# A 64-byte-offset layout for split weights, wider key matmuls, two-pass gates and float32r decode sums in a one-core decoder layer

## The chip, the cores and the metric

The kernel runs as one program on one core of one Trainium2 chip. The metric is device microseconds of the execution. A profiled execution gives the trace that is quoted below. Engines are named as the profile names them: PE (TensorE matmuls), PEld (TensorE weight loads), DVE (VectorE), ACT (ScalarE), POOL (GpSimd) and SP (SyncE, which here only issues DMAs).

## The reference

One inference step of a hybrid decoder layer for 256 prompt tokens and 8 sample tokens, 264 token columns in all, model width 2048, float32 throughout:

```python
xn = rmsnorm(x, g_mix)
z = xn @ w_in                       # RG-LRU group, mLSTM group, 4 + 4 gate columns
x = x + concat([y_rg, y_ml]) @ w_out
mk = rmsnorm(mem, g_mem) @ w_k      # 256 memory tokens, 4 heads of 512
mv = rmsnorm(mem, g_mem) @ w_v
q = rmsnorm(x, g_xa) @ w_xa_q       # prompt attends to mk, mv; samples to cache_mem_k, cache_mem_v
x = x + attention(q, k, v) @ w_xa_o
xf = rmsnorm(x, g_ffn)
x = x + (silu(xf @ w_ffn_gate) * (xf @ w_ffn_up)) @ w_ffn_down
y = rmsnorm(x, g_final)
```

Outputs are y for all tokens, the recurrent states, and mk and mv. Each of the 8 sample tokens attends to its own 256 cached keys and values in each of 4 heads: 32 pairs of head and sample.

## The kernel before

Tokens lie along the free dimension and features along the partitions, so an activation is 16 chunks of 128 features by 264 columns. Every large product is made to float32 accuracy from three float32r matmuls: each operand is split into a high part (a float32r copy) and a low part (the rest), and `mm3` (line 175) adds high·high, high weight·low token and low weight·high token into one PSUM bank. The moving operand is the token chunk (264 columns), the stationary one a 128x128 block of weights.

The weights are consumed in an ordered list of steps (`steps`, line 137). One step is one output block of 128 features: 2048 weight columns, 16 chunks, 48 matmuls. A step has a DMA of 1 MB into a raw tile (`load_piece`, line 142; three buffers), two splits of 1024 columns each (`split_half`, line 150: ACT copies raw to `wh`, DVE subtracts to get `wl`; four buffers of each), its matmuls, and an evacuation of the bank by DVE and ACT. The main loop (line 1200) runs, for step i: the load of a later piece, the evacuation of the step before, the split of step i+1, the matmuls of step i, and then side work (`pump`, line 207) until the planner's price clocks of DVE and ACT pass that of PE. Engine order is then made by a scheduler with a timeline of its own; only SP keeps the written order. Each engine works through its own instructions in order.

The steps in order are: 41 of `w_in`, 16 of `w_out`, 16 of `w_q`, 16 of `w_k` and 16 of `w_v` mixed by head, 16 of `w_o`, then the feed-forward part in three portions (gate and up projections 88, down projection 48).

Places that the change touches:

- Activations live in the tag `B` (line 100), 26 buffers. The largest tile that uses it has 4 chunks of 264 columns, so a buffer has 4224 bytes; its four rows of 1056 bytes start at 0, 32, 64 and 96 modulo 256 from the buffer's start, and neighbouring buffers differ by 128 modulo 256. `wh` and `wl` are 4096 bytes apart and a block of weights has 512, so every block starts at the same place modulo 256 (224, by the allocator's addresses).
- Step 8 (`w_in[8]`) holds the 8 gate columns in a block of 128 and takes the usual 48 matmuls; `evac_if` (line 501) reads rows 0 to 3 and 32 to 35.
- `w_k` steps: `proj` with 256 memory tokens, 48 matmuls of 256 columns; `evac_k` (line 986) copies the bank out, sends it to `o_k` and splits it (ACT, DVE).
- `w_v` steps: `pe_v` (line 1000) has the weights as the moving operand, 512 columns, and the memory tokens stationary.
- Decode attention: `dec_k` (line 927) issues on POOL's queue the DMAs of one pair's keys and values (512 KB each), then makes q·k products with one ACT and three DVE instructions into `acc`. `dec_v` (line 948) sums `acc` over the partitions with one float32 matmul against a matrix of ones, does the softmax, and weighs the values in four DVE instructions. Two pairs are under way at a time (`NFL`), and a DMA waits for a free buffer of `B`.
- In the 16 `w_k` steps and the decode work POOL's queue holds only DMA issues.

Of the kernel before, what the change touches and what calls it, by code (L numbers as in the profile page):

```python
# [10 lines left out]
F32 = mybir.dt.float32  # L11
F32R = mybir.dt.float32r
I32 = mybir.dt.int32
AF = mybir.ActivationFunctionType
# [3 lines left out]
P = 128  # L18
D = 2048
KC = D // P  # L20
T = 256
# [4 lines left out]
DFF = 5632  # L26
FPARTS = (16, 16, 12)
EPS = 1e-6
XSCALE = 512.0 ** -0.5
KSCALE = 128.0 ** -0.5  # L30

# [49 lines left out]
def layer_kernel(ctx: ExitStack, tc, xT, memT, vec, wrg, w_in, w_out, w_q, w_k, w_v, w_o,  # L81
# [28 lines left out]
    class Arr:  # L110


        def __init__(self, nb, w=N, dt=F32):
            self.t, self.nb, self.w, self.dt = {}, nb, w, dt
# [6 lines left out]
        def __call__(self, c):  # L121
            return self.tile(c // 4)[:, c % 4, :]

    class HL:
# [3 lines left out]
        def __call__(self, c):  # L128
            return self.h(c), self.l(c)

    NB, NT, NL, NFL = 26, 6, 3, 2
    SLACK = 0.5
    POOLC = (4, 5, 10, 11)
# [2 lines left out]

    steps = []
    LD, LS = 3, 1

    raws, splits = {}, {}  # L140

    def load_piece(i):
        if i >= len(steps) or i in raws:
            return
        src, cols = steps[i][0], steps[i][1]
        r = sb.tile([P, 2048], F32, tag="raw", bufs=3, name=nm("raw"))
        sp.dma_start(r[:, :cols], src)
        raws[i] = r

    def split_half(i, h, parts=1):  # L150
        if i >= len(steps):
            return
        cols = steps[i][1]
        lo, hi = h * 1024, min(cols, (h + 1) * 1024)
        wh = sb.tile([P, 1024], F32R, tag="wh", bufs=4, name=nm("wh"))
        wl = sb.tile([P, 1024], F32R, tag="wl", bufs=4, name=nm("wl"))
        r = raws[i]
        n = (hi - lo) // parts
        with tc.high_priority():
            for o in range(0, hi - lo, n):  # L160
                st["split"] = act.activation(wh[:, o: o + n], r[:, lo + o: lo + o + n], AF.Copy)
                dve.tensor_sub(wl[:, o: o + n], r[:, lo + o: lo + o + n], wh[:, o: o + n])
        splits[i, h] = (wh, wl)

    class W:
        def __init__(self, i):
            self.i = i

        def __call__(self, c, w=P):
            per = 1024 // w  # L170
            wh, wl = splits[self.i, c // per]
            o = (c % per) * w
            return wh[:, o: o + w], wl[:, o: o + w]

    def mm3(ps, a, b, start, stop):
        ah, al = a
# [49 lines left out]
    def bank(tag="mm"):  # L226
        return psm.tile([P, 512], F32, tag=tag, bufs=4, name=nm(tag))
# [3 lines left out]
    make_identity(nc, ident)  # L231
    ones = const.tile([P, P], F32, name="ones")
    dve.memset(ones, 1.0)
    warm_act = const.tile([P, 1], F32, name="warm_act")
    act.activation(warm_act, ones[:, 0:1], AF.Square)

# [14 lines left out]
    def V(name, j=0, w=1):  # L251
        o = _V[name][0] + j
        return vecs[:, o: o + w]
# [567 lines left out]
    proj(w_in[8], rx, evac_if)  # L821
    for j in range(8):
        proj(w_in[9 + j], rx, evac_qk(j))
    for j in range(8):
# [52 lines left out]
    def mem_gen():  # L877
        raw = Arr(KC, T)
        for i in range(4):
            pool_e.dma_start(raw.tile(i), memT[:, i * 4: i * 4 + 4, :])  # L880
        yield STEP
        yield STEP
        acc = ltmp(T)
        for c in range(KC):
            sumsq(acc, raw(c), c == 0)
            yield 0.35
        r = ltmp(T)
        yield STEP
        yield from rstd_from(acc, r, D)
        st["mem"] = HL(KC, T)  # L890
# [36 lines left out]
    def dec_k():  # L927
        for h in range(H):
            while qn["n"] < 4 * h + 4:
                yield STEP  # L930
            for b in range(NS):
                while infl["n"] >= NFL:
                    yield STEP
                infl["n"] += 1
                kc = B([P, 4, T])
                pool_e.dma_start(kc, kcT[h, b])  # L936
                w = sb.tile([P, 516], F32, tag="dw", bufs=2, name=nm("dw"))
                vc = B([P, 4, T])
                pool_e.dma_start(vc, vcT[h, b])
# [5 lines left out]
                pairs.append((h, b, w, vc))  # L945
                yield 1.1

    def dec_v():
        done, cur = 0, None
        while done < H * NS:  # L950
            nxt = None
            if pairs:
                nxt = pairs.pop(0)
                ps = bank("ax")
                pe.matmul(ps[:, :T], ones, nxt[2][:, 0:T], start=True, stop=True)
                nxt += (ps,)
            cur, todo = nxt, cur
            if todo is None:
                yield STEP
                continue  # L960
            h, b, w, vc, ps = todo
            mx, p = w[:, 512:513], w[:, T: 2 * T]
            dve.tensor_reduce(mx, ps[:, :T], axis=AX.X, op=OP.max)
            dve.tensor_scalar(mx, mx, -XSCALE, None, op0=OP.mult)
            act.activation(p, ps[:, :T], AF.Exp, scale=XSCALE, bias=mx, accum_out=ssm[:, h, b: b + 1])
            yield 0.5
            for c in range(4):
                dve.scalar_tensor_tensor(w[:, 0:T], vc[:, c, :], 1.0, p, op0=OP.mult, op1=OP.mult,
                                         accum_out=osm[:, 4 * h + c, b: b + 1])
# [16 lines left out]
    def evac_k(h, j):  # L986
        def f(ps):
            if j == 0:
                kv["k", h] = HL(4, T)
            t = tmp(T)  # L990
            act.activation(t, ps[:, :T], AF.Copy)
            pool_e.dma_start(o_k[:, 4 * h + j, :], t)
            kh, kl = kv["k", h](j)
            act.activation(kh, ps[:, :T], AF.Copy)
            dve.tensor_sub(kl, ps[:, :T], kh.bitcast(F32))
            if j == 3:
                st["att", h] = side(attend(h), 1)
        return f

    def pe_v(h, k4):  # L1000
        def f(i):
            if k4 == 0:
                kv["vps"] = [bank(), bank()]
            w = W(i)
            for c in range(4):
                kc = k4 * 4 + c
                mh, ml_ = rm(kc)
                wh, wl = w(c, 512)
                for tb in range(2):
                    ps = kv["vps"][tb]  # L1010
# [21 lines left out]
    def attend(h):  # L1032
# [42 lines left out]
        for c in range(4):  # L1075
# [9 lines left out]
            dve.tensor_sub(ol[:, T:N], x, oh[:, T:N].bitcast(F32))  # L1085
            yield 0.5

    for h in range(H):
        for j in range(4):
            proj(w_k[4 * h + j], rm, evac_k(h, j), n=T, need=("memg",))  # L1090
# [86 lines left out]
    def load_x(lo, hi):  # L1177
        sp.dma_start(xres[:, lo:hi, :], xT[:, lo:hi, :])  # L1178

    r = sb.tile([P, 2048], F32, tag="raw", bufs=3, name=nm("raw"))  # L1180
    raws[0] = r
    for h in range(4):
        if h < 2:
            load_x(2 * h, 2 * h + 2)
        sp.dma_start(r[:, h * 512: h * 512 + 512], w_in[0][:, h * 512: h * 512 + 512])  # L1185
    for q in range(1, 4):
        load_x(4 * q, 4 * q + 4)
        if q < 3:
# [157 lines left out]
```

## Time and profile before

| what | value |
| --- | --- |
| time, three runs | 1582.69, 1577.44, 1579.3 us; median 1579.3 us |
| profiled execution, first to last instruction (its span) | 1577.6 us; of the profiled execution only this is given, and the lowest timed run, 1577.44, lies at it |
| mean granted TensorE clock | 0.994 |
| PE matmuls in the trace | 12356 (a float32 matmul shows as two) |
| DMA | 207 GB/s mean, 325.97 MB |
| stage: w_k and w_v steps | 486.6 to 697.4 us |
| stage: feed-forward, final norm | 807 us to the end |

In the profile a PE record is the matmul with its pipeline, so records overlap: two that follow each other start about 121 ns apart while each lasts about 284 ns. A line L60 is the recording helper that issues nearly everything, so groups are told apart by their tiles. The chain of waits goes back from the last instruction to what released each step. Times of windows are us from the start of the span.

### The profile page before, as it was taken

The numbers are of one execution on the slowest core, as the hardware profiler recorded it, in microseconds if no ns is written. First come the engines' busy times: TensorE is split into PE (matmuls) and PEld (weight loads), VectorE is DVE, ScalarE is ACT, GpSimd is POOL, SyncE is SP. The second block draws the span as 40 slices with busy tenths as digits, with TensorE's granted clock in tenths as the row PEclk, the third lists the DMA queues.
The fourth block names the chain that finished last, engine by engine and source line by source line (L and its number), as shares of the span: only waits on it lengthen the run. The fifth ranks groups of instructions, "written<-read, shape, count | busy, mean of one in ns | idle before, by whom it ended". The sixth has DMA issues, their size and how long they took to land.

```text
span 1577.6 us, 29752 instructions
## 1 busy us (share of the span) xinstructions
PE 1560.9 (99%) x12356; PEld 1536.0 (97%) x12356; DVE 1047.3 (66%) x2019; ACT 779.2 (49%) x1217; POOL 74.9 (5%) x142
## 2 busy tenths in 40 slices
PE   9999999999999999999999999999999999999997
PEld 9999999999999889989999999999999999999997
DVE  7976878787689999856655555455555554555554
ACT  7465775564445555545444444333444433344463
POOL 0001210001012112000000000000000000000000
PEclk9999999999999999999999999999999999999999
DMA  8445875547689888554545555455445555555452
GB/s 311 154 174 171 303 262 202 189 159 260 247 298 353 314 330 302 178 182 180 187 163 185 188 181 173 182 187 186 174 178 185 188 181 174 180 188 188 153 180 97
DMA packets 55303, 325.97 MB, mean 207 GB/s; under 512 B 6688, under 2 KB 7120, under 8 KB 24448
## 3 DMA queue, kind: packets, MB, share of 16 engines
q1 hardware_dynamic: 39744, 270.68, 47.9%
q0 software_dynamic: 15136, 53.16, 9.2%
q8 instruction: 96, 1.57, 0.4%
q10 hardware_dynamic: 288, 0.23, 0.1%
q14 instruction: 39, 0.32, 0.1%
HBM read 312.78 MB, written 11.28 MB: 205 GB/s over the span
## 4 chain that ended last, share of the span: by engine, by line
PE 97%; ACT 1%; DVE 1%; DMA 0%; issue 0%; SPq 0%; DVEq 0%; ACTq 0%
PE mm L60 92%; PE ax L60 6%; DVE B L60 1%; ACT B L60 1%; DMA xres<-xT 0%; ACT wh L60 0%; ACT L60 0%; DVE wl L60 0%; DVE c L60 0%; DVEq L1323 0%; DVE xres L60 0%; ACT t L60 0%; SPq L1185 0%; ACT rstd L60 0%; SPq L1178 0%
## 5 line engine op out<-in xcount | busy, mean ns | idle before, releaser
L60 PE MATMUL mm<-B,wh 128*128 128x264 f32 (+1 forms) x7520 | 1380.0, 285 | 2.8 <-DVE B L60 2.8
L60 PEld LDWEIGHTS mm<-B,wh 128*128 128x128 f32 x7520 | 1166.8, 189 | 4.4 <-ACT cso L60 2.9
L60 PE MATMUL mm<-B,wl 128*128 128x264 f32 (+1 forms) x3760 | 1066.9, 284 | 1.2 <-DVE wl L60 1.2
L60 ACT ACTIVATE wh<-raw 128x1024 fp32r<-128x1024 f32 (+2 forms) x518 | 538.4, 1041 | 710.1 <-PE mm L60 584.1
L60 DVE TENSOR_TENSOR wl<-raw,wh 128x1024 fp32r<-128x1024 f32 (+2 forms) x518 | 620.7, 1200 | 370.0 <-ACT wh L60 361.8
L60 PEld LDWEIGHTS mm<-B,wl 128*128 128x128 f32 x3760 | 708.8, 189 | 1.6 <-DVE wl L60 1.4
L60 DVE TENSOR_TENSOR t<-mm,rstd 128x264 f32<-128x264 f32 x104 | 44.9, 432 | 57.5 <-PE mm L60 57.5
L60 PE MATMUL mm<-wh,B 128*128 128x512 f32 x256 | 83.0, 398 | 0.0
L60 DVE TENSOR_TENSOR xres<-xres,mm 128x264 f32<-128x264 f32 x80 | 34.3, 428 | 46.5 <-PE mm L60 46.5
L60 PEld LDWEIGHTS mm<-wh,B 128*128 128x128 f32 x256 | 48.4, 189 | 10.5
L60 DVE SCALAR_TENSOR_TENSOR dw<-B,dw 128x256 f32<-128x256 f32 x128 | 53.8, 420 | 3.2 <-ACT dw L60 2.2
L60 PE MATMUL mm<-wl,B 128*128 128x512 f32 x128 | 51.0, 398 | 0.0
L60 PE MATMUL ax<-B,B 128*128 128x256 f32 (+3 forms) x288 | 48.7, 312 | 0.0
L60 DVE SCALAR_TENSOR_TENSOR dw<-B,qsm,dw 128x256 f32<-128x256 f32 x96 | 45.9, 480 | 1.2 <-ACT dw L60 0.6
L60 PEld LDWEIGHTS ax<-B,B 128*128 128x128 f32 x288 | 40.7, 189 | 3.4 <-issue 0.7
L1238 POOL TENSOR_TENSOR B<-B,rstd 128x264 f32<-128x264 f32 x4 | 2.8, 739 | 866.0 <-ACT rstd L60 866.0
L60 ACT ACTIVATE B<-xres,vecs 128x264 fp32r<-128x264 f32 (+1 forms) x64 | 31.2, 504 | 2.5 <-DMA xres<-xT 1.3
L60 ACT ACTIVATE t<-xres 128x264 f32<-128x264 f32 x60 | 23.8, 416 | 15.3 <-DVE xres L60 15.3
L60 PEld LDWEIGHTS mm<-wl,B 128*128 128x128 f32 x128 | 24.1, 188 | 5.1
L936 POOL DMA_DIRECT2D B<-kcT x32 | 17.3, 541 | 209.9 <-DVE B L60 119.3
L60 DVE TENSOR_TENSOR acc_x<-acc_x,t 128x264 f32<-128x264 f32 x59 | 25.3, 428 | 0.8 <-ACT t L60 0.5
L60 DVE SCALAR_TENSOR_TENSOR B<-xres,vecs,B 128x264 fp32r<-128x264 f32 x48 | 22.7, 489 | 4.5 <-ACT B L60 4.5
(152 smaller groups left out, 701.3 us busy)
## 6 DMA issues: line engine op xcount, KB each, us to landing
raw<-w_gu SPq DMA_DIRECT2D x88, 1024.0 KB, 4.8
raw<-w_in SPq DMA_DIRECT2D x40, 1024.0 KB, 4.8
raw<-w_d SPq DMA_DIRECT2D x32, 1024.0 KB, 4.8
raw<-w_out SPq DMA_DIRECT2D x16, 1024.0 KB, 4.8
B<-kcT POOLq DMA_DIRECT2D x32, 512.0 KB, 7.0
raw<-w_q SPq DMA_DIRECT2D x16, 1024.0 KB, 6.6
B<-vcT POOLq DMA_DIRECT2D x32, 512.0 KB, 7.6
raw<-w_k SPq DMA_DIRECT2D x16, 1024.0 KB, 7.2
```

The source lines that it names most:

```text
L60: return f(*a, **k)
L936: pool_e.dma_start(kc, kcT[h, b])
L1238: e.tensor_mul(st["y"](c), st["y"](c), r)
```

## The change

Six edits:

1. Every tile of tag `B` now has 1088 columns (4352 bytes, 17 times 256), with the wanted shape cut out of it by `view`. All buffers so start at one place modulo 256.
2. `wh` and `wl` become one tile `W` of two groups of 1088 columns. A group starts with 16 columns of lead, then has four rows of 264: 128 columns of high part, 128 of low, 8 unused. A row of weights so starts 64 bytes after the token row that it meets, modulo 256, and moves on with it by 32 bytes per chunk. The split writes through a pattern of 2 x 4 x 128.
3. Raw pieces are loaded in halves of 1024 columns, five buffers in place of three whole ones.
4. The gate step has 64 columns of high part and 64 of low in one block of 128, and two matmuls per chunk; `evac_if` adds rows 64 to 67 and 96 to 99 to the results, four DVE instructions more.
5. The memory tokens are kept with high and low part side by side (`Side`), 512 columns; `pe_k` takes one matmul of 512 columns with the high weights and one of 256 with the low weights per chunk. `evac_k` copies one half on ACT, adds the other on DVE, and makes the low part of the key on POOL. `pe_v` reads its 512 moving columns as four rows of 128.
6. The decode sum is split: ACT copies `acc` to a float32r high part, POOL subtracts for the low part (`dr`), and PE sums with two float32r matmuls against `ones_r`. The products with the values are written over the value tile.

```diff
+SLOT = 1088
+ROW = 264
+LEAD = 16
...
-    def B(shape, dt=F32):
-        return sb.tile(shape, dt, tag="B", bufs=NB, name=nm("B"))
+    def B(shape, dt=F32, skip=0):
+        return view(sb.tile([P, SLOT], dt, tag="B", bufs=NB, name=nm("B")), shape, skip)
...
+        def both(self, c):
+            q, j = divmod(c, 2)
+            if q not in self.t:
+                self.t[q] = B([P, 2, 2 * T + 8], F32R, skip=16 * (q % 2))
+            return self.t[q][:, j, : 2 * T]
...
+        for h in range(0, cols, 1024):
+            if (i, h // 1024) not in raws:
+                w = min(1024, cols - h)
+                sp.dma_start(raw_half(i, h // 1024)[:, :w], src[:, h: h + w])
...
+        raws[i, h] = sb.tile([P, 1024], F32, tag="raw", bufs=5, name=nm("raw"))
...
-        wh = sb.tile([P, 1024], F32R, tag="wh", bufs=4, name=nm("wh"))
-        wl = sb.tile([P, 1024], F32R, tag="wl", bufs=4, name=nm("wl"))
+        w = sb.tile([P, 2, SLOT], F32R, tag="W", bufs=4, name=nm("W"))
+        ng = (hi - lo) // 512
+        rows = w[:, 0:ng, LEAD: LEAD + 4 * ROW].rearrange("p g (r x) -> p g r x", x=ROW)
...
-                st["split"] = act.activation(wh[:, o: o + n], r[:, lo + o: lo + o + n], AF.Copy)
-                dve.tensor_sub(wl[:, o: o + n], r[:, lo + o: lo + o + n], wh[:, o: o + n])
+                src, wh = raw[:, g, r, :], rows[:, g, r, 0:P]
+                low = rows[:, g, r, P: 2 * P]
+                if fused:
+                    wh, low, src = wh[:, :, :, 0:64], wh[:, :, :, 64:P], src[:, :, :, 0:64]
+                st["split"] = act.activation(wh, src, AF.Copy)
+                dve.tensor_sub(low, src, wh)
...
+        for o, x in ((64, li), (96, u)):
+            low = R(2)[0:4]
+            dve.tensor_mul(low, ps[o: o + 4, :N], rstd[o: o + 4, :])
+            dve.tensor_add(x, x, low)
...
+            pe.matmul(ps[:, :N], w(c)[0], xh, start=c == 0, stop=False)
+            pe.matmul(ps[:, :N], w(c)[0], xl, start=False, stop=c == KC - 1)
...
+                act.activation(wr[:, 0], acc, AF.Copy)
+                pool_e.tensor_sub(wr[:, 1], acc, wr[:, 0].bitcast(F32))
...
-                pe.matmul(ps[:, :T], ones, nxt[2][:, 0:T], start=True, stop=True)
+                for k, x in enumerate(nxt[4]):
+                    pe.matmul(ps[:, :T], ones_r, x, start=k == 0, stop=k == 1)
...
-            act.activation(t, ps[:, :T], AF.Copy)
+            act.activation(t, ps[:, T:], AF.Copy)
+            dve.tensor_add(t, t, ps[:, :T])
...
-            act.activation(kh, ps[:, :T], AF.Copy)
-            dve.tensor_sub(kl, ps[:, :T], kh.bitcast(F32))
+            act.activation(kh, t, AF.Copy)
+            pool_e.tensor_sub(kl, t, kh.bitcast(F32))
...
+            pe.matmul(ps, wh, st["mem"].both(c), start=c == 0, stop=last, skip_group_check=True)
+            if not last:
+                pe.matmul(ps[:, :T], wl, rm(c)[0], start=False, stop=False, skip_group_check=True)
```

On PE, the first key step, before. A `mm` tile is the PSUM bank; the first name behind the arrow is the moving tokens (two buffers, high and low), the second the weights; `ax_5982` is the sum of one decode pair, placed between.

```order
L60 MATMUL mm_6089<-B_4156,wh_6002 128x256
L60 MATMUL mm_6089<-B_4157,wh_6002 128x256
L60 MATMUL mm_6089<-B_4156,wl_6003 128x256
L60 MATMUL ax_5982<-dw_5914,ones 128x256
L60 MATMUL mm_6089<-B_4156,wh_6002 128x256
L60 MATMUL mm_6089<-B_4157,wh_6002 128x256
L60 MATMUL mm_6089<-B_4156,wl_6003 128x256
```

On PE, the same key step in the changed kernel.

```order
L63 MATMUL mm_6127<-B_4149,W_6038 128x512
L63 MATMUL mm_6127<-B_4149,W_6038 128x256
L63 MATMUL mm_6127<-B_4149,W_6038 128x512
L63 MATMUL mm_6127<-B_4149,W_6038 128x256
L63 MATMUL mm_6127<-B_4156,W_6038 128x512
L63 MATMUL mm_6127<-B_4156,W_6038 128x256
L63 MATMUL mm_6127<-B_4156,W_6038 128x512
L63 MATMUL mm_6127<-B_4156,W_6038 128x256
L63 MATMUL mm_6127<-B_4163,W_6038 128x512
L63 MATMUL ax_6014<-dr_5944,ones_r 128x256
L63 MATMUL mm_6127<-B_4163,W_6038 128x256
```

Three matmuls of 256 columns per chunk have become one of 512 and one of 256, and the decode sum reads `dr`, which POOL writes last; its second matmul stands further down.

On POOL, the queue in the decode work, before: each row is the issue of one DMA of keys (kcT) or values (vcT).

```order
L936 DMA B_5669<-kcT 128x1024
L939 DMA B_5672<-vcT 128x1024
L936 DMA B_5748<-kcT 128x1024
L939 DMA B_5751<-vcT 128x1024
L936 DMA B_5827<-kcT 128x1024
L939 DMA B_5830<-vcT 128x1024
```

On POOL, the same place in the changed kernel.

```order
L998 DMA B_5690<-vcT 128x1024
L994 DMA B_5769<-kcT 128x1024
L1005 TENSOR_TENSOR dr_5522<-dw_5521,dr_5522 128x256
L998 DMA B_5773<-vcT 128x1024
L994 DMA B_5852<-kcT 128x1024
L1005 TENSOR_TENSOR dr_5606<-dw_5605,dr_5606 128x256
L998 DMA B_5856<-vcT 128x1024
L1005 TENSOR_TENSOR dr_5689<-dw_5688,dr_5689 128x256
L1005 TENSOR_TENSOR dr_5772<-dw_5771,dr_5772 128x256
L994 DMA B_5941<-kcT 128x1024
```

The subtraction that makes the low part of one pair's `acc` now stands behind DMA issues of later pairs, each of which can wait for a buffer.

More of the change, by code (lines that the diff above doesn't have):

```diff
@@ L98, in nm, with view @@
         return f"{s}_{uid[0]}"
-    def B(shape, dt=F32):
-        return sb.tile(shape, dt, tag="B", bufs=NB, name=nm("B"))
+    def view(t, shape, skip=0):
+        v = t[:, skip: skip + int(np.prod(shape[1:]))]
+        if len(shape) == 2:
+            return v
+        names = "abcd"[:len(shape) - 1]
+        return v.rearrange(f"p ({' '.join(names)}) -> p {' '.join(names)}",
+                           **{c: int(n) for c, n in zip(names[1:], shape[2:])})
+    def B(shape, dt=F32, skip=0):
+        return view(sb.tile([P, SLOT], dt, tag="B", bufs=NB, name=nm("B")), shape, skip)
     def tmp(w=N, tag="t"):
@@ L129, in __call__, with __init__ @@
             return self.h(c), self.l(c)
+    class Side:
+        def __init__(self):
+            self.t = {}
+        def both(self, c):
[3 more added lines that the diff above has]
+            return self.t[q][:, j, : 2 * T]
+        def __call__(self, c):
+            b = self.both(c)
+            return b[:, :T], b[:, T:]
     NB, NT, NL, NFL = 26, 6, 3, 2
@@ L138, in layer_kernel, with raw_half @@
     LD, LS = 3, 1
+    GATES = 8
     raws, splits = {}, {}
     def load_piece(i):
-        if i >= len(steps) or i in raws:
+        if i >= len(steps):
             return
         src, cols = steps[i][0], steps[i][1]
-        r = sb.tile([P, 2048], F32, tag="raw", bufs=3, name=nm("raw"))
-        sp.dma_start(r[:, :cols], src)
-        raws[i] = r
+        for h in range(0, cols, 1024):
+            if (i, h // 1024) not in raws:
+                w = min(1024, cols - h)
+                sp.dma_start(raw_half(i, h // 1024)[:, :w], src[:, h: h + w])
+    def raw_half(i, h):
+        raws[i, h] = sb.tile([P, 1024], F32, tag="raw", bufs=5, name=nm("raw"))
+        return raws[i, h]
     def split_half(i, h, parts=1):
@@ L154, in split_half @@
         lo, hi = h * 1024, min(cols, (h + 1) * 1024)
-        wh = sb.tile([P, 1024], F32R, tag="wh", bufs=4, name=nm("wh"))
-        wl = sb.tile([P, 1024], F32R, tag="wl", bufs=4, name=nm("wl"))
-        r = raws[i]
-        n = (hi - lo) // parts
-        with tc.high_priority():
-            for o in range(0, hi - lo, n):
-                st["split"] = act.activation(wh[:, o: o + n], r[:, lo + o: lo + o + n], AF.Copy)
-                dve.tensor_sub(wl[:, o: o + n], r[:, lo + o: lo + o + n], wh[:, o: o + n])
-        splits[i, h] = (wh, wl)
+        w = sb.tile([P, 2, SLOT], F32R, tag="W", bufs=4, name=nm("W"))
+        ng = (hi - lo) // 512
+        rows = w[:, 0:ng, LEAD: LEAD + 4 * ROW].rearrange("p g (r x) -> p g r x", x=ROW)
+        raw = raws[i, h][:, : hi - lo].rearrange("p (g r x) -> p g r x", r=4, x=P)
+        pieces = [(slice(0, ng), slice(0, 4))]
+        if parts > 1:
+            pieces = [(slice(g, g + 1), slice(r, r + 8 // parts)) for g in range(ng) for r in range(0, 4, 8 // parts)]
+        fused = i == GATES
+        with tc.high_priority():
+            for g, r in pieces:
+                src, wh = raw[:, g, r, :], rows[:, g, r, 0:P]
[4 more added lines that the diff above has]
+                dve.tensor_sub(low, src, wh)
+        splits[i, h] = w
     class W:
@@ L167, in __init__, with __call__, wide @@
             self.i = i
[L169 to L173, printed above, removed]
+        def __call__(self, c):
+            w, g, o = splits[self.i, c // 8], c % 8 // 4, LEAD + c % 4 * ROW
+            return w[:, g, o: o + P], w[:, g, o + P: o + 2 * P]
+        def wide(self, c):
+            w = splits[self.i, c // 2][:, c % 2, LEAD: LEAD + 4 * ROW].rearrange("p (r x) -> p r x", x=ROW)
+            return w[:, :, 0:P], w[:, :, P: 2 * P]
     def mm3(ps, a, b, start, stop):
@@ L233, in layer_kernel @@
     dve.memset(ones, 1.0)
+    ones_r = const.tile([P, P], F32R, name="ones_r")
+    dve.tensor_copy(ones_r, ones)
     warm_act = const.tile([P, 1], F32, name="warm_act")
@@ L820, in layer_kernel, with pe_gates @@
         proj(w_in[n], rx, evac_rgx(n))
-    proj(w_in[8], rx, evac_if)
+    def pe_gates(i):
+        ps = bank()
+        w = W(i)
+        for c in range(KC):
+            xh, xl = rx(c)
+            pe.matmul(ps[:, :N], w(c)[0], xh, start=c == 0, stop=False)
+            pe.matmul(ps[:, :N], w(c)[0], xl, start=False, stop=c == KC - 1)
+        return ps
+    steps.append((w_in[8], 2048, pe_gates, evac_if, ()))
     for j in range(8):
@@ L889, in mem_gen @@
         yield from rstd_from(acc, r, D)
-        st["mem"] = HL(KC, T)
+        st["mem"] = Side()
         for c in range(KC):
@@ L936, in dec_k @@
                 pool_e.dma_start(kc, kcT[h, b])
-                w = sb.tile([P, 516], F32, tag="dw", bufs=2, name=nm("dw"))
+                w = sb.tile([P, 264], F32, tag="dw", bufs=2, name=nm("dw"))
+                wr = sb.tile([P, 2, T], F32R, tag="dr", bufs=2, name=nm("dr"))
                 vc = B([P, 4, T])
@@ L944, in dec_k @@
                     dve.scalar_tensor_tensor(acc, kc[:, c, :], q[c], acc, op0=OP.mult, op1=OP.add)
-                pairs.append((h, b, w, vc))
+                act.activation(wr[:, 0], acc, AF.Copy)
+                pool_e.tensor_sub(wr[:, 1], acc, wr[:, 0].bitcast(F32))
+                pairs.append((h, b, w, vc, (wr[:, 0], wr[:, 1])))
                 yield 1.1
@@ L960, in dec_v @@
                 continue
-            h, b, w, vc, ps = todo
-            mx, p = w[:, 512:513], w[:, T: 2 * T]
+            h, b, w, vc, _, ps = todo
+            mx, p = w[:, T: T + 1], w[:, 0:T]
             dve.tensor_reduce(mx, ps[:, :T], axis=AX.X, op=OP.max)
@@ L1007, in f @@
                 mh, ml_ = rm(kc)
-                wh, wl = w(c, 512)
+                wh, wl = w.wide(c)
                 for tb in range(2):
-                    ps = kv["vps"][tb]
+                    ps = kv["vps"][tb].rearrange("p (r x) -> p r x", x=P)
                     s = slice(tb * P, tb * P + P)
@@ L1086, in attend, with pe_k @@
             yield 0.5
+    def pe_k(i):
+        ps = bank()
+        w = W(i)
+        for c in range(KC):
+            wh, wl = w(c)
+            last = c == KC - 1
+            if last:
+                pe.matmul(ps[:, :T], wl, rm(c)[0], start=False, stop=False, skip_group_check=True)
+            pe.matmul(ps, wh, st["mem"].both(c), start=c == 0, stop=last, skip_group_check=True)
+            if not last:
+                pe.matmul(ps[:, :T], wl, rm(c)[0], start=False, stop=False, skip_group_check=True)
+        return ps
     for h in range(H):
         for j in range(4):
-            proj(w_k[4 * h + j], rm, evac_k(h, j), n=T, need=("memg",))
+            steps.append((w_k[4 * h + j], 2048, pe_k, evac_k(h, j), ("memg",)))
         for k4 in range(4):
@@ L1178, in load_x @@
         sp.dma_start(xres[:, lo:hi, :], xT[:, lo:hi, :])
-    r = sb.tile([P, 2048], F32, tag="raw", bufs=3, name=nm("raw"))
-    raws[0] = r
     for h in range(4):
@@ L1184, in layer_kernel @@
             load_x(2 * h, 2 * h + 2)
-        sp.dma_start(r[:, h * 512: h * 512 + 512], w_in[0][:, h * 512: h * 512 + 512])
+        r = raws[0, h // 2] if h % 2 else raw_half(0, h // 2)
+        sp.dma_start(r[:, h % 2 * 512: h % 2 * 512 + 512], w_in[0][:, h * 512: h * 512 + 512])
     for q in range(1, 4):
```

2 lines of the change are left out of this document (1 added, 1 removed).

## The prediction

> **What bounds the kernel now.** I read the engine totals first, then the chain of waits, and then what PE itself waits for.
>
> ```profile
> span 1577.6 us, 29752 instructions
> PE 1560.9 (99%) x12356; PEld 1536.0 (97%) x12356; DVE 1047.3 (66%) x2019; ACT 779.2 (49%) x1217; POOL 74.9 (5%) x142
> ...
> 807.26 756.09 PE mm L60 x6233
> ...
> PE mm L60 <- DVE B L60: 2.8, 1, 2.8
> PE ax L60 <- ACT wh L60: 1.4, 1, 1.4
> PE mm L60 <- DVE wl L60: 1.2, 1, 1.2
> ```
>
> The first two rows: PE is busy through 99% of the span, DVE through 66%. The third, from the chain of waits in the feed-forward stage, is one unbroken stretch of 6233 matmuls, and 756.09 / 6233 = 121.3 ns each. The last three are waits of PE (us in all, times, longest); they come to 5.4 us. So the time is a count of matmuls times their spacing, and nothing else ends last for long. An edit helps if it removes matmuls or shortens their spacing, and hurts if it makes PE wait.
>
> The groups by shape (busy us, mean ns of a record) and two ranges over 900 to 1200 us (shortest, median and longest record in ns):
>
> ```profile
> L60 PE MATMUL mm<-B,wh 128*128 128x264 f32 x7008 | 1286.5, 285 | 2.8 <-DVE B L60 2.8
> L60 PE MATMUL mm<-B,wl 128*128 128x264 f32 x3504 | 994.9, 284 | 1.2 <-DVE wl L60 1.2
> L60 PE MATMUL mm<-B,wh 128*128 128x256 f32 x512 | 93.5, 283 | 0.0
> L60 PE MATMUL mm<-wh,B 128*128 128x512 f32 x256 | 83.0, 398 | 0.0
> L60 PE MATMUL mm<-B,wl 128*128 128x256 f32 x256 | 72.0, 281 | 0.0
> ...
> L60 PE MATMUL mm<-B,wl x826: 278/283/289, 899.7 to 1199.9; 128*128 128x264 f32 x166
> L60 PE MATMUL mm<-B,wh x1650: 278/284/290, 899.9 to 1199.8; 128*128 128x264 f32 x184
> ```
>
> A record lasts longer than its spacing because matmuls are pipelined: 284 against 121.3 ns, about 163 ns more. I take that 163 off every record to get a spacing: 120 and 118 ns for the two kinds of 256 columns, 235 for 512. The ranges show that equal matmuls differ by up to 12 ns, with PE never waiting.
>
> **The change part by part.** The sum is made against the profiled execution's span of 1577.6 us; the median, 1579.3, lies 1.7 us above it, which I add at the end.
>
> *Layout (edits 1 and 2).* It touches every 264-column matmul, 16 chunks of three in each step. The relation that the change fixes, weights 64 bytes behind the tokens modulo 256, already occurs in the kernel before: by the allocator's addresses its buffers start at 96 or at 224 and a row is 32 further on, so the third row of a buffer at 96 starts at 160, and the weights, always at 224, stand 64 behind it. I looked for it in the output projection, where high and low tokens both lie in buffers that start at 96.
>
> ```profile
> 727.26 0.41 PE L60 MATMUL mm<-B,wh 128*128 128x264 f32 x2
> ...
> 727.63 0.40 PE L60 MATMUL mm<-B,wh 128*128 128x264 f32 x2
> ...
> 727.99 0.41 PE L60 MATMUL mm<-B,wh 128*128 128x264 f32 x2
> ...
> L60 PE MATMUL mm<-B,wh x2: 281/282/283, 727.6 to 727.7; 128*128 128x264 f32 x2
> L60 PE MATMUL mm<-B,wl x1: 286/286/286, 727.9 to 727.9; 128*128 128x264 f32 x1
> ```
>
> The timeline has that chunk at 727.63, with 0.36 us to the next and 0.37 before it; the two rows below are its three records, 281 + 283 + 286 = 850 ns. Three medians make 2 x 284 + 283 = 851, three means 2 x 285 + 284 = 854. So the fixed relation is worth 1 to 4 ns per chunk; I take 2, since chunks start 0.36 and 0.37 us apart in turn. 10,464 / 3 = 3488 chunks keep three matmuls: 3488 x 2 = **7.0 us less**, ends 3.5 and 14. The trace can't tell whether the relation counts or the address alone; both lead to this chunk. A larger gain is not excluded: one matmul in three falling to the shortest record, 278, would bring 6 x 3488 = 20.9 us.
>
> *Gates (4).* One step of 48 matmuls becomes one of 32: 16 x 0.121 = **1.9 us less**.
>
> *Keys (5).* Before, 512 x 120 + 256 x 118 ns = 91.6 us; after, 256 x 235 + 256 x 118 = 90.4 us: **1.3 us less** before rounding. The low-token half rides in the same pass, so only the few ns that a second matmul costs beyond its columns go. The value steps keep their 384 matmuls; no row shows 512 columns read as four rows of 128, and I take 0, with 11 ns either way (the spread of equal matmuls) for the ends, 4 us.
>
> *Decode sums (6).*
>
> ```profile
> 446.57 1.01 DVE L60 SCALAR_TENSOR_TENSOR dw<-B,qsm,dw 128x256 f32<-128x256 f32 x2
> ...
> 450.18 0.59 PE L60 MATMUL ax<-dw,ones 128*128 128x256 f32 x2
> 450.43 0.47 PE L60 MATMUL mm<-B,wl 128*128 128x264 f32 x1
> 450.74 0.41 PE L60 MATMUL mm<-B,wh 128*128 128x264 f32 x2
> ```
>
> From 450.18 to 450.74 PE starts the sum and one ordinary matmul; 0.56 less 0.12 leaves 0.44 us for a float32 sum. Two float32r matmuls of 256 columns take 2 x 0.119 = 0.238. That is 0.20 less for each of 32 pairs: **6.5 us less**. It holds only while the sum's new operand is ready. Before, `acc` is complete at 447.58 (first row) and the sum starts at 450.18: 2.6 us of cover.
>
> ```profile
> L60 ACT ACTIVATE t<-B 128x256 f32<-128x256 f32 x15 | 5.1, 406 | 0.0
> L1238 POOL TENSOR_TENSOR B<-B,rstd x4: 734/738/746, 1568.8 to 1570.9; 128x264 f32<-128x264 f32 x4
> L60 DVE SCALAR_TENSOR_TENSOR t<-t,t 4x264 f32<-4x264 f32 x8 | 3.3, 418 | 0.2
> L60 ACT ACTIVATE wh<-raw 128x1024 fp32r<-128x1024 f32 x496 | 525.7, 1061 | 700.0 <-PE mm L60 574.6 <-issue 105.9 <-ACT B L60 13.9
> L60 DVE TENSOR_TENSOR wl<-raw,wh 128x1024 fp32r<-128x1024 f32 x496 | 606.9, 1225 | 369.2 <-ACT wh L60 361.0 <-PE mm L60 0.9
> raw<-w_gu SPq DMA_DIRECT2D x88, 1024.0 KB, 4.8
> L147 SPq DMA_DIRECT2D raw<-w_gu x88: 327/328/328, 773.0 to 1466.8; - x88
> ```
>
> The new chain in front of the sum is an ACT copy of 256 columns, 0.41 us, and a POOL subtraction, 738 x 256 / 264 = 0.72 us: 1.13 of the 2.6 us, 1.5 left. If POOL's queue held it up, PE would stop with all its later matmuls behind the sum.
>
> *Costed at nothing.* The 32 ACT copies, and the 16 DVE adds that take the place of the subtractions in `evac_k`, lie beside PE; the 16 POOL subtractions there make the key's low part, needed a head later. Four instructions of 0.42 us in `evac_if` are 1.7 us of DVE once, within a step of 48 x 0.121 = 5.8 us; uncovered they cost 1.7. The split in 128-column pieces handles the same elements. A half step is 2.9 us, and it needs 1.06 of ACT and 1.23 of DVE, so even half as much again stays under PE. With `wh` and `wl` in one tile a buffer comes free with its last reader, still four halves deep. Twice as many raw DMAs cost SP 0.33 us more per step, and SP does nothing else; a whole piece lands in 4.8 us, under a step of 5.8, and five halves keep 2.5 steps ahead in place of 3. If that cover failed, PE would wait about 1 us a step.
>
> The **sum** is −7.0 − 1.9 − 1.3 − 6.5 = −16.7: span 1560.9, and 1562.6 on the scale of the median. Its own range: gain from layout 3.5 to 14, values ±4, evacuation up to 1.7: 1552 to 1572.
>
> **The rivals.**
>
> *All short.* The layout could bring every 264-column matmul to the shortest record, 278 ns: 6 x 7008 + 5 x 3504 ns = 59.6 us, with the other terms (9.7) 1510 us. For it: 278 occurs in both ranges. Against it: the one chunk of this relation has records of 281, 283 and 286, and the excess grows with the columns: 398 − 284 = 114 ns over 248 columns is 0.46 ns a column, so most of the 121 looks like plain streaming. The Trainium skill, in "TensorE: Matmul & The Clock Gate", Back-to-back issue gap, gives N / 2.4 + 2.5 ns, which would be 112.5 here, an estimate from that page; the trace disagrees with 121.3 at a granted clock of 1.00 (window row below).
>
> *Layout moves nothing.* The spread could follow something else than addresses, such as the order of reads and loads. Then 9.7 us go: 1569.6. For it: only one place was read, and its 850 against 851 is within rounding. Against: equal matmuls differ though PE never waits, and the pattern of 0.36 and 0.37 repeats chunk by chunk. The Trainium skill, "SBUF — State Buffer", Who interferes with whom, gives PE independent ports for moving rows and weight loads and says it waits on no engine; by that, offsets would change nothing, and the spread from 278 to 290 speaks against it without settling it.
>
> *POOL takes from DVE.*
>
> ```profile
> 440.00:640.00 200.00, 200.00 (x1378) 186.49 (x1376) 181.55 (x496) 110.54 (x205) 36.72 (x68) 1.00 0.84 314
> ...
> POOL B L936 <- DVE dw L60: 23.0, 8, 5.7
> POOL B L939 <- DVE dw L60: 20.4, 7, 4.5
> ```
>
> The window row gives busy us of PE, PEld, DVE, ACT, POOL, then granted clock and DMA share. DVE is at 181.55 of 200 us in the decode stage. If each of the 48 POOL subtractions stopped DVE for its whole 0.72 us, 34.6 us came on top: 216 us of DVE in 200, and PE would wait some 16 us, which eats the gain: 1579, no change. For it: this is the one stage where DVE is nearly full. Against: a DVE that is 91% busy has most of its work due later than now. The Trainium skill has the mechanism on the same page and section: a DVE instruction with two SBUF inputs contends with a GpSimd one that reads SBUF; no run shown here has the two together.
>
> *POOL's queue takes the place of the float32 sum: slower.* A subtraction for a pair stands in POOL's queue behind DMA issues of later pairs, which wait for buffers. The two rows above are such waits: 23.0 us in 8 and 20.4 in 7. With a keys issue and a values issue ahead of each subtraction, some 8 subtractions share 43.4 us, and 1.5 us of cover each takes 12: 31 us of PE standing still, 1562.6 + 31 = 1594. It decides as soon as a wait ahead of a subtraction exceeds 1.5 us, and the mean of these is 2.9. Against it: they wait for DVE to finish an earlier pair, which mostly is done before this pair's `acc` is; a wait that ends before `acc` is complete costs nothing.
>
> **How the numbers follow.** Forecast 0.58, all short 0.06, layout nothing 0.16, POOL against DVE 0.09, queue 0.11. Faster by over 0.3% (4.7 us, about what a measurement of this kernel can tell from no change) are the first three: 0.80; same 0.09; slower 0.11. The range holds the forecast and the second layout case; its low end takes the larger gain of 20.9 us (1579.3 − 9.7 − 20.9 = 1548.7, with the lower bounds of the values 1545) and its high end reaches to the edge of the POOL case, 1579. Outside stay all short and the queue, 0.17.
>
> **What would show it.** In the feed-forward stretch the spacing should be 120.6 ns in place of 121.3, with a narrower range than 278 to 290; unchanged medians mean that the layout did nothing. Decode sums should be pairs of records near 281 ns with the next matmul 0.24 us after the first; the gate step 32 matmuls; the keys 398 and 281. PE rows waiting for POOL `dr` would bring the queue; a mean of the split's subtractions clearly above 1225 ns between 440 and 640 us, with PE waiting for `W`, brings POOL against DVE. The forecast is wrong if the spacing moves by more than 2 ns, or if PE's waits exceed some 10 us.

## The result and the profile after

The changed kernel takes 1566.24 us (median of 4 runs, 1564.94 to 1566.95) against 1579.3 us before: 13.1 us less, a ratio of 0.9913 with a 95% interval of 0.9899 to 0.9927. The prediction's sum was 1562.6.

The page of the changed kernel (busy us, share, instructions), and the two longest pieces of its chain of waits (start, length, work):

```profile
span 1563.9 us, 30136 instructions
PE 1545.7 (99%) x12084; PEld 1511.2 (97%) x12084; DVE 1057.5 (68%) x2024; ACT 786.2 (50%) x1249; POOL 124.5 (8%) x190
```

```profile
703.34 86.86 PE mm L63 x714
797.83 751.42 PE mm L63 x6232
```

All that PE waited for (us in all, times, longest):

```profile
PE mm L63 <- DVE B L63: 2.2, 1, 2.2
PE mm L63 <- DVE W L63: 2.0, 2, 1.4
PE ax L63 <- ACT W L63: 1.7, 1, 1.7
PE mm L63 <- DVE ones L63: 1.1, 1, 1.1
PE ax L63 <- DVE c L63: 0.7, 1, 0.7
PE mm L63 <- DVE c L63: 0.3, 1, 0.3
```

Two window rows, in the columns of the prediction's, and the range of the feed-forward matmuls' records in the second window:

```profile
440.00:640.00 200.00, 200.00 (x1212) 178.37 (x1211) 184.88 (x463) 118.53 (x222) 74.48 (x105) 1.00 0.86 312
900.00:1200.00 300.00, 300.00 (x2491) 300.00 (x2490) 163.68 (x192) 120.83 (x140) 0.00 (x0) 1.00 0.55 182
```

```profile
L63 PE MATMUL mm<-B,W x2491: 278/283/288, 899.8 to 1199.9; 128*128 128x264 f32 x192
```

PE is still the bound, and its waits are 8.0 us in all, none of them on POOL. The last stretch of feed-forward matmuls splits the gain. It starts at 797.83 in place of 807.26, so 9.4 us went in the stages ahead of it (up to some 2 of them by the clock of the first 260 us, see under the experiments); it lasts 751.42 in place of 756.09, so 4.7 us went in it (it holds one record less, 0.12 us of that). Per matmul that is 751.42 / 6232 = 120.57 ns in place of 121.30, or 2.2 ns per chunk of three. The 714 matmuls of the output projection (`w_o`) went the other way: 86.86 / 714 = 121.65 ns, where the same stage before has this row:

```profile
708.77 90.84 PE mm L60 x750
```

90.84 / 750 is 121.12 ns. So the layout shortens one stage and lengthens another.

The groups that the change made or altered:

```profile
L63 PE MATMUL mm<-B,W 128*128 128x264 f32 x10496 | 1285.8, 284 | 4.3 <-DVE B L63 2.2 <-DVE W L63 2.0
L63 PE MATMUL mm<-B,W 128*128 128x512 f32 x256 | 89.9, 395 | 0.0
L63 PE MATMUL mm<-B,W 128*128 128x256 f32 x256 | 69.3, 280 | 0.0
L63 DVE SCALAR_TENSOR_TENSOR B<-B,dw 128x256 f32<-128x256 f32 x128 | 55.6, 489 | 4.0 <-ACT dw L63 4.0
L63 DVE SCALAR_TENSOR_TENSOR dw<-B,qsm,dw 128x256 f32<-128x256 f32 x96 | 49.7, 526 | 0.4
L1005 POOL TENSOR_TENSOR dr<-dw,dr 128x256 fp32r<-128x256 f32 x32 | 35.0, 1097 | 106.8 <-ACT dr L63 105.6 <-DVE W L63 1.1
```

One decode pair in the timeline (start, length):

```profile
430.14 0.42 ACT L63 ACTIVATE dr<-dw 128x256 fp32r<-128x256 f32 x1 [0.59 <-DVE dw L63]
430.64 1.20 POOL L1005 TENSOR_TENSOR dr<-dw,dr 128x256 fp32r<-128x256 f32 x1 [12.50 <-ACT dr L63]
...
434.31 0.40 PE L63 MATMUL ax<-dr,ones_r 128*128 128x256 f32 x2
434.54 0.64 PE L63 MATMUL mm<-B,W 128*128 128x264 f32 x4
```

The last two rows are the decode sum as foreseen: 434.54 − 434.31 = 0.23 us for this pair, where the float32 sum took 0.44. Its operand is ready at 430.64 + 1.20 = 431.84, 2.5 us ahead. POOL's subtraction takes 1097 ns on the mean where 0.72 us was estimated, and before it POOL mostly waited for ACT's copy (105.6 of 106.8 us, in 20 waits).

### The profile page after: what moved, and what is told of

Read it like the earlier page. It is cut to its first block, busy times and chain, and to the rows that moved or that the text cites. A ratio compares the mean times of both kernels' runs of the same rounds, so it can differ in the third digit from the quotient of the medians.

```text
span 1563.9 us, 30136 instructions
## 1 busy us (share of the span) xinstructions
PE 1545.7 (99%) x12084; PEld 1511.2 (97%) x12084; DVE 1057.5 (68%) x2024; ACT 786.2 (50%) x1249; POOL 124.5 (8%) x190
## 4 chain that ended last, share of the span: by engine, by line
PE 96%; DVE 2%; ACT 1%; DMA 0%; issue 0%; SPq 0%; DVEq 0%; ACTq 0%
PE mm L63 91%; PE ax L63 5%; DVE B L63 1%; ACT B L63 1%; DVE W L63 0%; DMA xres<-xT 0%; ACT W L63 0%; ACT L63 0%; DVE xres L63 0%; DVE c L63 0%; ACT t L63 0%; SPq L1260 0%; ACT rstd L63 0%; SPq L1254 0%; DVE acc_x L63 0%
## 5 line engine op out<-in xcount | busy, mean ns | idle before, releaser
L63 PE MATMUL mm<-B,W 128*128 128x264 f32 (+2 forms) x11008 | 1378.3, 286 | 4.3 <-DVE B L63 2.2
L63 PEld LDWEIGHTS mm<-B,W 128*128 128x128 f32 x11008 | 1354.8, 188 | 16.3 <-DVE W L63 2.5
L63 ACT ACTIVATE W<-raw 128x1024 fp32r<-128x1024 f32 (+2 forms) x518 | 536.5, 1037 | 667.4 <-PE mm L63 460.6
L63 DVE TENSOR_TENSOR W<-raw,W 128x1024 fp32r<-128x1024 f32 (+2 forms) x518 | 621.3, 1201 | 366.0 <-ACT W L63 364.9
L63 PE MATMUL mm<-W,B 128*128 128x512 f32 x384 | 92.0, 394 | 0.0
L63 PEld LDWEIGHTS mm<-W,B 128*128 128x128 f32 x384 | 71.0, 188 | 15.3
L63 DVE SCALAR_TENSOR_TENSOR B<-B,dw 128x256 f32<-128x256 f32 x128 | 55.6, 489 | 4.0 <-ACT dw L63 4.0
L1005 POOL TENSOR_TENSOR dr<-dw,dr 128x256 fp32r<-128x256 f32 x32 | 35.0, 1097 | 106.8 <-ACT dr L63 105.6
L63 ACT ACTIVATE B<-t 128x264 fp32r<-128x264 f32 (+1 forms) x60 | 24.2, 409 | 4.0 <-DVE t L63 3.8
L63 ACT ACTIVATE t<-t 128x264 f32<-128x264 f32 (+1 forms) x61 | 24.8, 406 | 1.3 <-DVE t L63 1.2
```

Of the source, the lines that this page charges most:

```text
L63: return f(*a, **k)
L1005: pool_e.tensor_sub(wr[:, 1], acc, wr[:, 0].bitcast(F32))
```

## The experiments

Each kernel is the changed one with the edit shown. Times are medians; where only one run was made it is called a single time. The main reading is the start and the length of the feed-forward stretch in the chain of waits. Its length repeats to a few hundredths of a microsecond between kernels that share a layout. Its start doesn't: 797.83 in two kernels and 796.66 in a third, all with the offset of 64. The kernel with the offset of 192, traced twice, starts it at 794.06 and at 792.30, and the granted clock of the first 260 us differs too, 0.98 and 0.99 (the number before the last two):

```profile
0.00:260.00 260.00, 253.67 (x1964) 248.23 (x1965) 209.78 (x555) 164.49 (x332) 24.20 (x50) 0.98 0.69 233
0.00:260.00 260.00, 252.93 (x1979) 247.04 (x1979) 210.29 (x557) 165.91 (x334) 24.15 (x50) 0.99 0.70 234
```

So starts are compared to about 2 us only, unless this clock agrees. It is 0.97 for the kernel before, 0.98 for the changed kernel, for "Old layout", "Float32 sum", "Subtraction on DVE" and 128, and 0.99 for "Old keys and gates" and 64 moved.

### The parts undone one at a time

**Old layout.** Rows of 1056 columns, high and low weights each contiguous:

```diff
-SLOT = 1088
+SLOT = 1056
...
-        w = sb.tile([P, 2, SLOT], F32R, tag="W", bufs=4, name=nm("W"))
+        w = sb.tile([P, 2, 1024], F32R, tag="W", bufs=4, name=nm("W"))
...
-            w, g, o = splits[self.i, c // 8], c % 8 // 4, LEAD + c % 4 * ROW
-            return w[:, g, o: o + P], w[:, g, o + P: o + 2 * P]
+            w, o = splits[self.i, c // 8], c % 8 * P
+            return w[:, 0, o: o + P], w[:, 1, o: o + P]
```

> The changed kernel with edits 1 and 2 undone (buffers of 1056 columns, high and low weights contiguous, every block of weights at one place modulo 256). Theory 'layout': the matmul spacing of the feed-forward stretch goes from the changed kernel's 120.57 ns back to 121.3, the shares of w_in, w_out, w_q and w_o hardly move, and the time is 4 to 5 us above the changed kernel's 1566.2, about 1571. My prediction's size of this term would make it 7 us, 1573. Rival 'not the layout' (half-size loads or the strided splits quicken PE): the spacing stays at 120.6 and the time at 1566.

1570.49 us (1569.88 to 1573.95), 4.2 above the changed kernel, as the theory had it. The chain of waits:

```profile
705.91 86.38 PE mm L61 x714
799.96 755.21 PE mm L61 x6232
```

The stretch is 3.8 us longer, 121.18 ns a matmul, and starts 2.1 later; the 714 of the output projection are 0.5 shorter. Half-size loads, which this kernel keeps, are therefore not what quickened PE. The splits write contiguous blocks here, so this run doesn't part the layout from strided splits; the sweep of offsets below does, since all its kernels have strided splits and their stretches take 748.00 to 765.25 us. Not all comes back: at equal counts the stretch had gained 4.5 us (756.09 − 0.12 − 751.42), and the other 0.8 isn't explained.

**Float32 sum.**

```diff
-                act.activation(wr[:, 0], acc, AF.Copy)
-                pool_e.tensor_sub(wr[:, 1], acc, wr[:, 0].bitcast(F32))
...
-                for k, x in enumerate(nxt[4]):
-                    pe.matmul(ps[:, :T], ones_r, x, start=k == 0, stop=k == 1)
+                pe.matmul(ps[:, :T], ones, nxt[2][:, 0:T], start=True, stop=True)
```

> The changed kernel with the decode sum in float32 again, without the ACT copy and the POOL subtraction ahead of it. Theory 'PE pays the sum': each of the 32 sums takes 0.43 to 0.44 us of PE in place of 0.24, the time is 6.5 us above the changed kernel's, about 1572.7. Rival 'the new chain costs what the sum saves': PE or DVE wait less without the POOL subtractions, and the time moves by less than 3 us. On either, DVE's multiply-adds of the decode work lose their long records (longest 1410 and 1916 ns now), if POOL's subtractions cause them.

1571.66 us (1570.8 to 1573.11), 5.4 above. The chain of waits, and two groups:

```profile
804.91 751.42 PE mm L63 x6232
```

```profile
L63 DVE SCALAR_TENSOR_TENSOR dw<-B,qsm,dw 128x256 f32<-128x256 f32 x96 | 49.4, 516 | 1.5 <-ACT dw L63 1.1
L63 DVE SCALAR_TENSOR_TENSOR B<-B,dw 128x256 f32<-128x256 f32 x128 | 47.7, 428 | 4.2 <-ACT dw L63 4.2
```

The stretch starts 7.1 us later and has the same length to the hundredth: the whole loss lies ahead of it, 5.4 to 7.1 us, around the 6.5 that the sums were priced at. The value products are back at 428 ns; the key products only came from 526 to 516. The longest records fell to 1291 and 1305 ns and didn't go, as was expected of them. POOL still makes the keys' low parts here, 16 subtractions, but it does so in "Subtraction on DVE" below as well, where the mean is 485: what keeps the 516 up isn't shown.

**Old keys and gates.**

```diff
-            steps.append((w_k[4 * h + j], 2048, pe_k, evac_k(h, j), ("memg",)))
+            proj(w_k[4 * h + j], rm, evac_k(h, j), n=T, need=("memg",))
...
-    steps.append((w_in[8], 2048, pe_gates, evac_if, ()))
+    proj(w_in[8], rx, evac_if)
```

(with the additions in `evac_k` and `evac_if` taken out.)

> The changed kernel with edits 4 and 5 undone for PE (48 matmuls in the gate step, three matmuls of 256 columns per chunk of keys). The gate step's 16 matmuls should cost 1.9 us in the w_in stage; the keys 1.3 us by my prediction, and 0.7 us by what the two traces leave over when sums and gates are taken out. Together 2.6 to 3.2 us, about 1569. Rival 'wide matmuls save more' (each matmul costs several ns beyond its columns): 256 fewer matmuls at 8 ns and more, 2 us or more for the keys, over 1570.

1569.88 us (1567.33 to 1571.12), 3.6 above. The chain of waits:

```profile
799.65 751.42 PE mm L63 x6232
```

The stretch starts 1.8 us later, at the higher early clock of 0.99, so 1.8 is rather too little. By the times alone, 3.6 with a range of 1567.33 to 1571.12, the expected 2.6 to 3.2 can't be told from the rival's "over 1570". For the keys the starts of the records in the two traces tell more. From the start of a key matmul to the next it is 118.4 ns on the mean before, and 232.5 (512 columns) and 117.5 (256) in the changed kernel, so 768 x 118.4 − 256 x 350.0 ns = 1.3 us, and not the 2 and more of the rival.

**Subtraction on DVE.**

```diff
-                pool_e.tensor_sub(wr[:, 1], acc, wr[:, 0].bitcast(F32))
+                dve.tensor_sub(wr[:, 1], acc, wr[:, 0].bitcast(F32))
```

> The changed kernel with the decode subtraction (32 of them) on DVE in place of POOL. Theory 'POOL and DVE exclude each other': POOL's subtraction shows 1097 ns on the mean with a shortest of 729, and DVE's multiply-adds up to 1916 with medians of 418 and 478, because each waits out the other's whole instruction; without it the mean of the multiply-adds falls from 489 and 526 to about 420 and 480, and only the 16 subtractions of the keys still collide. Rival 'the long records come from writing over the value tile': they stay. PE waits for neither now, so both expect the time within 2 us of 1566.2.

1565.45 us (1565.34 to 1568.6), the same as the changed kernel. The groups, and the stretch in the chain of waits, as in the changed kernel:

```profile
797.83 751.42 PE mm L63 x6232
...
L63 DVE SCALAR_TENSOR_TENSOR B<-B,dw 128x256 f32<-128x256 f32 x128 | 47.6, 427 | 1.2 <-ACT dw L63 1.2
L63 DVE SCALAR_TENSOR_TENSOR dw<-B,qsm,dw 128x256 f32<-128x256 f32 x96 | 46.2, 485 | 0.6
L63 DVE TENSOR_TENSOR dr<-dw,dr 128x256 fp32r<-128x256 f32 x32 | 14.5, 457 | 0.0
```

The products still write over the value tile, and yet their means fell from 489 to 427 and from 526 to 485: the long records came from POOL. The ranges say how, those of the changed kernel first, then the products of the kernel before: medians stay, and a few records are very long.

```profile
L63 DVE SCALAR_TENSOR_TENSOR B<-B,dw x128: 399/418/1916, 425.5 to 681.1; 128x256 f32<-128x256 f32 x128
L63 DVE SCALAR_TENSOR_TENSOR dw<-B,qsm,dw x96: 460/478/1410, 404.4 to 670.0; 128x256 f32<-128x256 f32 x96
L1005 POOL TENSOR_TENSOR dr<-dw,dr x32: 729/1073/1744, 412.7 to 672.2; 128x256 fp32r<-128x256 f32 x32
...
L60 DVE SCALAR_TENSOR_TENSOR dw<-B,dw x128: 406/419/428, 427.7 to 660.5; 128x256 f32<-128x256 f32 x128
L60 DVE SCALAR_TENSOR_TENSOR dw<-B,qsm,dw x96: 473/480/488, 406.6 to 649.2; 128x256 f32<-128x256 f32 x96
```

Those records fit an instruction that waits out another's length. The Trainium skill, "SBUF — State Buffer", Who interferes with whom, says that a DVE instruction with two SBUF inputs and a GpSimd one that reads SBUF exclude each other; the fall from 489 to 427 ns agrees. DVE lost 128 x 62 + 96 x 41 ns = 11.9 us to it, 0.37 us for each of the 32 subtractions, and PE none of that: the stretch starts at 797.83 in both kernels, and PE's waits are 8.0 and 7.7 us.

### Which offset, and why

One constant sets it, 8 columns to 32 bytes; for larger offsets the tokens are moved instead:

```diff
-LEAD = 16
+LEAD = 0
...
-            self.t[q] = B([P, min(4, self.nb), self.w], self.dt)
+            self.t[q] = B([P, min(4, self.nb), self.w], self.dt, skip=24)
```

Lead and token skip in columns: 24 and 8 (64, moved); 0 and 0 (0); 24 and 0 (96); 0 and 24 (160); 32 and 0 (128); 8 and 0 (32); 0 and 16 (192). `Side` has the same skip.

> The changed kernel with tokens and weights both moved by 32 bytes, the relation of 64 kept. Theory 'relation' (the spacing depends on where a block of weights starts relative to the token row): the unbroken stretch of 6232 feed-forward matmuls takes 751.42 us as in the changed kernel, to within 0.1. Rival 'absolute place' (the start of the token row modulo 256 by itself counts): row sums change, since in the changed kernel rows at 0, 32, 64, 224 take 365.0, 361.7, 360.0, 360.1 ns per chunk and four other rows are now used; the stretch moves by 1 us or more.

> Weights start at the same place modulo 256 as the tokens (no lead). By 'relation', from the chunk of the kernel before that had this relation (row at 224, 361.1 ns per chunk): 6232 x 361.1 / 3 = 750.1 us for the stretch. Rival 'even rows' (what counts is only that high and low tokens and weights step by the same 32 bytes from row to row): 751.4 whatever the offset. Rival 'a clash of equal places': over 756, as before the change or worse.

> Weights 96 bytes behind the tokens. By 'relation', from the chunk of before with it (row at 128, 368.2 ns): 764.9 us for the stretch, 13.5 above the changed kernel. By 'even rows': 751.4.

> Weights 160 bytes behind the tokens (tokens moved by 96, no lead). By 'relation', from the chunk of before with it (row at 64, 356.7 ns, the shortest of all): 740.9 us for the stretch and about 16 us off the whole time, 1550. By 'even rows': 751.4 and no change. In between if a chunk's time also depends on the chunk ahead of it.

The chain of waits of each, first 64 moved:

```profile
796.66 751.42 PE mm L63 x6232
```

At 0:

```profile
798.65 758.32 PE mm L63 x6232
```

At 96:

```profile
803.47 765.25 PE mm L63 x6232
```

At 160:

```profile
799.11 751.49 PE mm L63 x6232
```

Moved by 32 bytes with the relation kept, the stretch is the same to the hundredth: in this stage the absolute place, as far as a move of 32 bytes can show it, is out. Changing the relation moves it by up to 13.8 us: "even rows" is out. But reading the size from one chunk of the old kernel worked only for 96 (764.9 expected, 765.25 measured); 0 came 8 us worse than expected and 160 came 10.6 worse. Single times: 1564.35, 1574.12, 1585.12 and 1566.87 us, with 1579.48 for the kernel before.

> Weights 128 bytes behind the tokens. Theory 'three loads' (a matmul's spacing follows the relation between its own token row and the weights that are loaded next; in a chunk two loads stand at the offset and the third 32 further on, or 160 further where a group ends; each relation has one mean spacing): from the means in the four offsets so far, 120.6 ns for 128, 120.3 for 160, 123.4 for 32: 2 x 120.6 + 0.75 x 120.3 + 0.25 x 123.4 = 362.3 ns per chunk, 752.5 us for the stretch of 6232. Rival 'state' (a matmul's time also hangs on those ahead of it, so that relations don't add): off by more than 3 us either way.

> Weights 32 bytes behind the tokens. By 'three loads': 2 x 123.4 + 0.75 x 119.7 + 0.25 x 121.5 = 366.9 ns per chunk, 762.2 us for the stretch. By 'state': off by more than 3 us.

> Weights 192 bytes behind the tokens (tokens moved by 64, no lead). By 'three loads': 2 x 121.5 + 0.75 x 120.0 + 0.25 x 123.4 = 363.9 ns per chunk, 755.9 us for the stretch. By 'state': off by more than 3 us. An offset below 751.4 would be a better choice than 64.

The chain of waits at 128:

```profile
802.93 751.45 PE mm L63 x6232
```

At 32:

```profile
795.57 751.46 PE mm L63 x6232
```

At 192:

```profile
794.06 748.00 PE mm L63 x6232
```

"Three loads" held for 128 (752.5 expected, 1.1 us off) and fell for 32 (762.2) and 192 (755.9). Its rival, that matmuls hang on those ahead of them, takes these two, but gives no number. What the row of offsets shows is a plateau: 32, 64, 128 and 160 all lie between 751.42 and 751.49, with 0 and 96 above it and 192 below. Single times: 1570.77, 1563.41 and 1558.32 us, against 1582.03 before. At 128 the stretch starts 5.1 us later than at 64, so the whole time doesn't follow the stretch alone.

The plateau is one of the feed-forward stage. The output projection's 714 matmuls, in the chains at 32, at 64 moved and at 0:

```profile
701.84 86.09 PE mm L63 x714
702.06 86.91 PE mm L63 x714
704.13 86.84 PE mm L63 x714
```

They take 86.11 us at 128, 86.14 at 160 and 87.64 at 96. So here 32, 128 and 160 still gain, 120.6 ns a matmul, while 64 (86.86, moved 86.91) takes 121.7, as 0 does: the relation alone doesn't set the spacing, and the 64 that the change chose is not the safest place of the plateau.

> The offset of 192 once more, timed against the kernel before. If the feed-forward stretch is set by the layout alone it takes 748.0 us again, to 0.1, and the time is about 1559, 7 us under the changed kernel's 1566.2 and 1.3% under the kernel before. If the one look was chance: the stretch returns to 751.4 or the time to 1565 and more.

1558.15 us (1556.59 to 1561.44), ratio to the kernel before 0.9854 (0.9834 to 0.9874): 8.1 us under the changed kernel, with the two intervals apart. The chain of waits:

```profile
698.94 85.75 PE mm L63 x714
792.30 748.00 PE mm L63 x6232
```

The stretch is 748.00 again, and here the output projection gains too (85.75 against 86.86). This version, the changed kernel with weights 192 bytes behind the tokens, beats both.

## Why the prediction was right, and where its sizes were off

- **PE is the bound and the time is a sum of spacings.** Right: waits of PE 8.0 us after, and the three undone parts give 4.2 + 5.4 + 3.6 = 13.2 us by their medians, where 13.1 were gained. The runs of each kernel spread over 2 to 4 us, so the agreement to 0.1 is chance.
- **Decode sums, 6.5 us.** Right: 0.23 us in the pair of the timeline, 5.4 us by the median and 7.1 by the start of the stretch.
- **Gates and keys, 1.9 + 1.3.** Right: 3.2 together, against 1.8 by the start and 3.6 by the median of the run; the keys are 1.3 by the starts of their matmuls, and 16 matmuls fewer at 0.121 are the gates.
- **Layout, 7.0 us.** The term that was mis-sized: 4.2 us. Its step "10,464 / 3 = 3488 chunks" gave every chunk the 2 ns of one. The feed-forward stretch did give 2.2 ns a chunk, 4.7 us, but the output projection lost 0.53 ns a matmul against before. And the step behind it, that one chunk of the old kernel tells what its relation is worth everywhere, doesn't hold: the offsets 0 and 160, read in the same way, came out 8 and 11 us wrong. That 64 came out near was partly luck. The prediction's own sign, that unchanged medians mean the layout did nothing, was wrong as well: the records kept a median of 283 ns and a range of 278 to 288, while their spacing fell from 121.30 to 120.57 ns.
- **Costed at nothing.** Right in sum: PE's waits grew by under 1 us (7.1 to 8.0, small ones included).
- **All short.** Out: the shortest records stay 278, medians 283. The offset that is best here reaches 748.00 / 6232 = 120.03 ns.
- **Layout moves nothing.** Out, by the old layout and by the sweep of offsets.
- **POOL takes from DVE.** The mechanism is there, with 11.9 us of DVE by the subtraction moved to DVE, 0.37 us for each subtraction where 0.72 was supposed; the consequence isn't. DVE's busy time in the window rose from 181.55 to 184.88 of 200 us and not to 216, and the decode work was spread: its last product starts at 681.1 in place of 660.5, and no PE instruction stood still for it.
- **POOL's queue.** Didn't occur: POOL waited for ACT's copy of `acc` 105.6 us in all, PE for `dr` never, and the pair shown had 2.5 us of cover left.

## What to carry to other kernels

Where PE never waits, price a change by counts times spacing, stage by stage, and read the spacing of a long unbroken stretch of the chain, which repeats to hundredths of a microsecond and shows a 0.5% effect that times hardly resolve. An address offset between moving rows and weights is worth a sweep of all eight places on the chip; what one place in an old trace says of it doesn't carry over. An engine that loses time to another cost nothing here, where what it feeds had slack, so look for who waits and not for who got slower.

## What the runs showed of the hardware

The spacing of float32r matmuls of 264 columns depends on where the weights lie relative to the moving row, modulo 256 bytes. In the feed-forward stage it goes from 120.03 ns (192) over 120.57 (32, 64, 128, 160) and 121.68 (0) to 122.79 (96), each from the stretch of 6232, and a move of both by 32 bytes changes nothing there. The Trainium skill, "SBUF — State Buffer", Who interferes with whom, gives PE independent read ports for moving rows and for weight loads and lets it wait on no engine. By that a spread of 2.3% with the offset alone isn't to be expected, and the measurement decides. What happens inside is open. The sequence matters and not the pair alone: four offsets meet at one value in the feed-forward stage, and one of them, 64, takes 121.65 ns in the output projection, where the other three take 120.6. A layout in which all three loads of a chunk stand at the same offset wasn't tried, and neither was 224.
